# Latent attention: the place of the maxima, the turn, the shift row and the gates

## The chip, the cores and the metric

The kernel runs on one core of one Trainium2 chip. The metric is the device time of one execution in microseconds (us); the reference points are three timed runs and one profiled execution of the kernel before. The engines are TensorE (PE in the profile, its weight loads PEld), VectorE (DVE), ScalarE (ACT), GpSimd (POOL) and SyncE (SP, which here issues DMAs).

## The reference, cut to what matters

A backbone of two layers over 1024 latent and 256 context tokens, model width 1024, float32. Layer 0 is a windowed attention, layer 1 a latent attention with 16 heads. The change touches only layer 1's attention and what follows it:

```python
def attend(qn, qr, kn, kr, v):
    s = (einsum("bqhd,bkhd->bhqk", qn, kn)      # 64 columns of a head
         + einsum("bqhd,bkd->bhqk", qr, kr)) * scale   # 32 rotated columns, keys shared by the heads
    p = softmax(s, axis=-1)
    return einsum("bhqk,bkhd->bqhd", p, v)
...
ox = attend(...)                    # 1024 queries against 1280 keys (context and latent)
yx = (ox * silu(gx)) @ w_out        # the gate, then the projection
x = x + gate_x * yx                 # and a last RMSNorm
```

## The kernel before, in words

Layer 1's attention is cut into 16 units. Unit `i` has one pair of heads (`i // 2`) and one half of the queries (512, `i % 2`). A unit goes over the 1280 keys in ten chunks of 128 (`NT = 10`). Inside a block called `in_order` each engine gets its instructions in the order in which the program issues them; nothing is reordered, so the place of a line in the unit loop is its place in the engine's queue.

For a chunk `c`, `score(c)` (line 1343) makes ten products into two PSUM banks, one for each head: five terms (high and low parts of the keys against the queries, the rotated part, and a last term that also adds the negated maximum of each query through extra rows of `q`). ScalarE takes the exponential of both banks at once (1347) and GpSimd adds it into a running sum `acc` (1351, 1353). The banks are 3 and 4 for even chunks, 5 and 6 for odd ones. `PV` (1360) multiplies five chunks at a time by the values, in two column halves of 64, into bank 7.

The maxima must be known before a unit's first exponential. So unit `nu`, the next one, has its maxima made during unit `u`, from rough scores of the high parts: `nu.top(PIECES[c])` (1305), four products of 512 keys (or eight of 256) into two of the banks 0 to 2, which go round (`topb`), and two reduces on VectorE (1311, 1313). After the last chunk and the last `PV`, `nu.turn` reduces the partial maxima (1316) and transposes them to a row on TensorE (1318), and `nu.shift` spreads that row into `q`: one head on VectorE (1323), the other in four pieces on ScalarE (1330). The turn's bank is 5 (`psd`) if a projection follows, else one of `topb`.

Finishing the unit before (`pu`) lies inside unit `u`: at chunk 5 `fin2` sums `acc` over its partitions on TensorE (1371) and copies it (1373); `fin3(0)` and, after the turn, `fin3(1)` take the reciprocal (1377) and multiply the output by it (1378), each for 256 queries; `fin4` multiplies by the gate on VectorE (1382) and stores the result (1384).

Between units TensorE may get a projection that fills the turn: K of the next pair after units 0, 2, ... 12 (`make_K`, lines 126 to 128, cast on ScalarE at 121, subtracted on VectorE at 122), V of the next four heads after units 3, 7 and 11 (`make_V`, copied by ScalarE at 1257). After units 1, 5, 9, 13 and 14 there is none. These projections use the same banks 0 to 2 (`fillb`, set to `topb`'s place). `nnu.prep` (1290 to 1295) loads the queries of the unit after the next; `fin` (1364, 1366) copies bank 7 out and loads the gate. `wo_fill` cuts pieces of the output weight on ScalarE and GpSimd (121, 122), one a unit, two in units 6, 12 and 13. Behind unit 15 come the output tiles (`out_tiles`), whose first needs unit 14's gated output (`fetch_out`, `cut_out`).

The unit loop before:

```python
if c == 0:
    u.score(0, 0, 4)
    u.score(1, 0, 4)
if c > 1:
    u.score(c)
if nu:
    nu.top(PIECES[c])
if c < 2:
    u.score(c, 4, 5)
```

Of the kernel before, what the change touches and what calls it, by code (L numbers as in the profile page):

```python
# [9 lines left out]
F32 = mybir.dt.float32  # L10
# [49 lines left out]
def kernel(ctx: ExitStack, tc: tile.TileContext, t, out, dbg=None):  # L60
    nc = tc.nc
# [57 lines left out]
    def split(hi, lo, src, lo_eng=None):  # L119

        nc.scalar.copy(hi, src)  # L121
        (lo_eng or nc.vector).tensor_sub(lo, src, hi.bitcast(F32))  # L122
# [1153 lines left out]
    class UnitB:  # L1276
# [38 lines left out]
        def turn(self, bank):  # L1315
            nc.vector.reduce_max(shp(self.mx, 2, 64)[:, :, 32:36], self.mxp, AX.X, negate=True)
            self.pm = bank
            nc.tensor.transpose(self.pm[0:100, 0:128], self.mx[:, 0:100], ident)

        def shift(self, engs):  # L1320
            for r, eng in zip((slice(32, 36), slice(96, 100)), engs):
                if eng is nc.vector:
                    eng.tensor_tensor(
                        shp(self.q[r, 3], 4, 128), self.pm[r, 0:128].unsqueeze(1).to_broadcast([4, 4, 128]),
                        ident[r, r].unsqueeze(2).to_broadcast([4, 4, 128]), ALU.mult,
                    )
                else:
                    for b in range(4):
                        o = self.q[r, 3, b * 128 : b * 128 + 128]
                        eng.activation(o, self.pm[r, 0:128], AF.Copy, scale=ident[r, r.start + b : r.start + b + 1])  # L1330

        def score(self, c, i0=0, i1=5):


            q, kt = self.q, self.kt
            cs = slice(c * 128, c * 128 + 128)
            b = 3 + 2 * (c % 2)
            terms = ((kt, 0, 0, 64), (kt, 0, 1, 64), (kt, 1, 0, 64), (KR, 0, 2, 64), (KR, 1, 3, 36))
            for i in range(i0, i1):
                k, s, sq, n = terms[i]  # L1340
                for e in range(2):
                    r = slice(64 * e, 64 * e + n)
                    nc.tensor.matmul(PB[:, b + e, :], k[r, s, cs], q[r, sq], start=i == 0, stop=i == 4)  # L1343
            if i1 < 5:
                return
            E = self.E[c] = shp(Er.next(), 2, 512)
            nc.scalar.activation(E, PB[:, b : b + 2, :], AF.Exp)  # L1347
            acc = shp(self.acc, 2, 512)
            eng = nc.vector if self.i == NU - 1 and c > 4 else nc.gpsimd
            if c == 1:  # L1350
                eng.tensor_add(acc, self.E[0], E)
            elif c:
                eng.tensor_add(acc, acc, E)  # L1353
# [8 lines left out]
        def fin(self):  # L1362
            self.o = otr.next()
            nc.scalar.copy(self.o, PB[:, 7, :])
            self.gt = glr.next()
            load(out=self.gt.bitcast(F32), in_=g1_d[self.pair, :, self.ts])

        def fin2(self):
            acc = shp(self.acc, 2, 512)
            for e, r in enumerate(HALF):  # L1370
                nc.tensor.matmul(psd[r, :], ones, acc[:, e], start=True, stop=True)  # L1371
            self.rec = self.acc[:, 0:512]
            nc.scalar.copy(self.rec, psd)

        def fin3(self, j):
            js = slice(256 * j, 256 * j + 256)
            nc.vector.reciprocal(self.rec[:, js], self.rec[:, js])
            nc.vector.tensor_mul(self.o[:, js], self.o[:, js], self.rec[:, js])

        def fin4(self, c0=0, c1=512):  # L1380
            cs = slice(c0, c1)
            nc.vector.tensor_mul(self.o[:, cs], self.o[:, cs], self.gt[:, cs].bitcast(F32))
            t0 = self.ts.start
            load(out=og_d[self.pair, :, t0 + c0 : t0 + c1], in_=self.o[:, cs])

# [29 lines left out]
        load(out=x, in_=x1_d[256 + ti * 128 : 384 + ti * 128, :])  # L1415
        return o, x

    def cut_out(f, eng=None):
        o, x = f
        og = shp(ogr1.next(), 2, 8, 128)  # L1420
        for h in range(2):
            hs = slice(4 * h, 4 * h + 4)
            split(og[:, 0, hs], og[:, 1, hs], o[:, hs].bitcast(F32), eng)
        return og, x

    def out_tiles(ready, got):
# [66 lines left out]
    for b in range(4):  # L1493
        for i in range(3):
            units[0].top([(b, i)], (PB[:, 2 * i, :], PB[:, 2 * i + 1, :]))
        next(gs[b])
        next(gs[b])
        if b == 3:
            units[0].turn(psd)
            units[0].shift((nc.vector, nc.vector))  # L1500
        next(gs[b])
        if b == 1:
            units[1].prep()
    nc.scalar.activation(const[:, 1:2], const[:, 1:2], AF.Exp)
    wo_fill = wo_pieces()
    for ui, u in enumerate(units):
# [3 lines left out]
        for c in range(NT):  # L1510
            if c == 5:
                if pu:
                    pu.fin2()
                u.PV(0, 5)
                if pu:
                    pu.fin3(0)
                if pu and nu is None:
                    pu.fin4(0, 256)
                    first = fetch_out(0)
                    pu.fin3(1)  # L1520
                    pu.fin4(256, 512)
# [12 lines left out]
            if nu is None and c == 0:  # L1534
                load2(out=gx1, in_=gate_d[1, 0, :].partition_broadcast(128))
                load2(out=fg, in_=t["final_g"].partition_broadcast(128))
        if nnu:
            nnu.prep()
        u.PV(5, NT)
        if nu:  # L1540
            filled = u.half == 0 and u.pair < 7 or ui % 4 == 3
            nu.turn(psd if filled else topb())
            if pu:
                pu.fin3(1)
# [93 lines left out]
```

## Time and profile before

| | |
|---|---|
| median of 3 runs | 1580.59 us (1579.82 to 1583.61) |
| the profiled execution | 1582.15 us |
| its span, first to last instruction | 1580.3 us |
| mean granted TensorE clock | 0.99 |
| busy: PE, DVE, ACT, POOL | 1522.8, 1015.2, 734.9, 775.4 us |
| the units, first score of unit 0 to the first output tile | 1004.05 to 1485.82 us of the span |

A row of the timeline has the start in us from the start of the span, the duration, the engine, the line, the operation, what it writes and reads, the count, and in brackets how long the engine stood before it and what ended that. Rows that follow each other without a gap are merged, so a row of five adds has the time of all five. The chain of work is followed back from the last instruction; its shares say which engine the end waited for. Busy PE is not PE at its peak: where a stretch of the same products takes longer than elsewhere, PE stood, even if the row shows little idle time.

### The profile page before, as it was taken

What the parts mean: (1) busy time and instruction counts of PE and PEld (TensorE: products, weight loads), DVE (VectorE), ACT (ScalarE), POOL (GpSimd) and SP (SyncE); (2) the same over time, 40 slices, a digit from 0 to 9 for tenths busy, and PEclk for the clock granted to TensorE, in tenths of its full rate; (3) what the DMA queues carried; (4) which work ended last, traced back from release to release, by engine and by line L of the source; (5) the groups of instructions that cost most, each with busy time, mean ns of one, the idle gap of its engine ahead of it and who ended that gap; (6) DMA issues with size and microseconds to landing.
All of it is one profiled execution on the core that took longest, in us unless ns stands there. A gap on an engine that the chain in (4) does not pass through costs nothing.

```text
span 1580.3 us, 24759 instructions
## 1 busy us (share of the span) xinstructions
PE 1522.8 (96%) x9026; PEld 1189.2 (75%) x9026; DVE 1015.2 (64%) x1895; ACT 734.9 (47%) x1433; POOL 775.4 (49%) x722
## 2 busy tenths in 40 slices
PE   6899999989999999998999999999999999999998
PEld 2788888778888888886987888766766666766687
DVE  2666868737767887777725202567678678677644
ACT  2512212238877777776523432344445444544422
POOL 2653446315554434444318340477677677688200
PEclk8999999989999999999999999999999999999999
DMA  8535644473333333316304841401122112111442
GB/s 301 175 118 183 196 144 171 144 223 108 114 111 94 97 94 94 94 55 222 92 16 145 308 129 54 117 15 50 44 68 71 44 44 87 44 45 37 140 160 80
DMA packets 123842, 178.91 MB, mean 113 GB/s; under 512 B 11708, under 2 KB 71996, under 8 KB 123720
## 3 DMA queue, kind: packets, MB, share of 16 engines
q1 hardware_dynamic: 116440, 166.40, 33.2%
q10 hardware_dynamic: 7280, 10.92, 2.3%
q8 instruction: 71, 1.16, 0.3%
q14 instruction: 51, 0.42, 0.1%
HBM read 131.13 MB, written 46.15 MB: 112 GB/s over the span
## 4 chain that ended last, share of the span: by engine, by line
PE 83%; DVE 5%; DMA 3%; POOL 3%; issue 3%; ACT 3%; SPq 0%; POOLq 0%; DVEq 0%; ACTq 0%
PE PB L126 14%; PE PB L127 13%; PE PB L128 13%; PE PB L1343 12%; PE PB L1360 9%; PE PB L1305 5%; PE PB L570 5%; PE PB L560 4%; PE PB L533 2%; PE PB L534 2%; PE PB L1371 1%; DMA arena_f<-a_w_in 1%; DMA arena_f<-x 1%; DVE arena_f L344 1%; POOL arena_r L122 1%
## 5 line engine op out<-in xcount | busy, mean ns | idle before, releaser
L126 PE MATMUL PB<-arena_r 128*128 128x512 f32 (+2 forms) x1312 | 475.7, 363 | 3.4 <-ACT arena_r L205 2.1
L127 PE MATMUL PB<-arena_r 128*128 128x512 f32 (+2 forms) x1312 | 469.5, 358 | 3.2 <-POOL arena_r L727 2.3
L128 PE MATMUL PB<-arena_r 128*128 128x512 f32 (+2 forms) x1312 | 469.2, 358 | 0.2 <-DVE arena_r L122 0.2
L1353 POOL TENSOR_TENSOR arena_f<-arena_f 128x1024 f32<-128x1024 f32 x123 | 294.6, 2395 | 18.8 <-ACT arena_f L1347 11.6
L126 PEld LDWEIGHTS PB<-arena_r 128*128 128x128 f32 x1312 | 250.4, 191 | 48.2 <-issue 6.9
L127 PEld LDWEIGHTS PB<-arena_r 128*128 128x128 f32 x1312 | 249.9, 191 | 37.8 <-POOL arena_r L727 2.8
L128 PEld LDWEIGHTS PB<-arena_r 128*128 128x128 f32 x1312 | 249.6, 190 | 35.4 <-DVE arena_r L122 0.4
L1311 DVE TENSOR_REDUCE krF<-PB 128x1 f32<-128x512 f32 (+1 forms) x264 | 167.2, 678 | 112.2 <-PE PB L1305 111.8
L1347 ACT ACTIVATE arena_f<-PB 128x1024 f32<-128x1024 f32 x160 | 164.3, 1027 | 157.2 <-PE PB L1343 154.5
L1343 PE MATMUL PB<-arena_r 64*128 64x512 f32 (+1 forms) x1600 | 220.0, 395 | 1.0 <-ACT arena_f L1347 0.9
L122 POOL TENSOR_TENSOR arena_r<-arena_f,arena_r 128x512 fp32r<-128x512 f32 x96 | 131.5, 1382 | 166.7 <-ACT arena_r L121 152.8
L1343 PEld LDWEIGHTS PB<-arena_r 64*128 64x128 f32 (+1 forms) x1600 | 159.4, 184 | 41.5 <-issue 13.3
L122 DVE TENSOR_TENSOR arena_r<-PB,arena_r 128x512 fp32r<-128x512 f32 (+2 forms) x215 | 140.1, 663 | 76.8 <-ACT arena_r L121 75.1
L540 DVE CUSTOM_DVE_ANT_0 arena_f<-PB,arena_f,small 128x256 f32<-128x256 f32 (+1 forms) x288 | 145.4, 524 | 32.6 <-PE PB L534 25.7
L121 ACT CAST arena_r<-PB 128x512 fp32r<-128x512 f32 (+2 forms) x215 | 120.0, 565 | 55.2 <-PE PB L560 40.9
L1360 PE MATMUL PB<-arena_f 128*64 128x512 f32 x640 | 143.6, 595 | 0.0
L541 ACT ACTIVATE arena_f<-arena_f,small 128x640 f32<-128x640 f32 (+2 forms) x160 | 118.9, 743 | 27.8 <-DVE small L540 26.7
L570 PE MATMUL PB<-arena_r 128*128 128x512 f32 x336 | 121.8, 438 | 4.7 <-ACT arena_f L581 4.1
L344 DVE SCALAR_TENSOR_TENSOR arena_f<-arena_f,small 128x512 f32<-128x512 f32 x98 | 116.2, 1232 | 3.9 <-DMA arena_f<-ada_w 3.5
L1305 PE MATMUL PB<-arena_r 64*128 64x512 f32 (+1 forms) x768 | 112.3, 360 | 6.5 <-DVE krF L1311 5.8
L1360 PEld LDWEIGHTS PB<-arena_f 128*64 128x64 f32 x640 | 44.4, 137 | 84.3 <-issue 82.0
L560 PE MATMUL PB<-ident,arena_f 128*128 128x128 f32 x672 | 105.8, 274 | 0.4 <-ACT arena_f L541 0.3
(165 smaller groups left out, 1892.8 us busy)
## 6 DMA issues: line engine op xcount, KB each, us to landing
arena_r<-q_d SPq DMA_DIRECT2D x148, 128.0 KB, 2.8
arena_f<-ada_w SPq DMA_DIRECT2D x64, 256.0 KB, 3.2
arena_f<-a_w_in SPq DMA_DIRECT2D x40, 256.0 KB, 3.0
arena_f<-ada_w SPq DMA_DIRECT2D x16, 512.0 KB, 7.2
arena_f<-x SPq DMA_DIRECT2D x16, 512.0 KB, 3.7
q_d<-arena_f SPq DMA_DIRECT2D x16, 512.0 KB, 3.2
qn_d<-arena_f SPq DMA_DIRECT2D x16, 512.0 KB, 5.7
arena_r<-qn_d SPq DMA_DIRECT2D x16, 512.0 KB, 5.8
```

The source lines that it names most:

```text
L122: (lo_eng or nc.vector).tensor_sub(lo, src, hi.bitcast(F32))
L126: nc.tensor.matmul(o, ah, bh, start=first, stop=False)
L127: nc.tensor.matmul(o, al, bh, start=False, stop=False)
L128: nc.tensor.matmul(o, ah, bl, start=False, stop=last)
L560: nc.tensor.transpose(pt[:, h, :], self.Ps[h][:, ci * 128 : ci * 128 + 128], ident)
L570: nc.tensor.matmul(self.pv, V[:, self.chunks[ci], self.g, :], PT[:, s], start=ci == 0 and s == 0, stop=ci == self.m - 1 and s == 1,)
L1305: nc.tensor.matmul(bank[:, o : o + n], self.q[r, s, bs], k[r, 0, n0 : n0 + n], start=s == 0, stop=s == 2)
L1311: nc.vector.reduce_max(self.mxp[:, e, b : b + 1, i], bank[:, 0:n], AX.X)
L1343: nc.tensor.matmul(PB[:, b + e, :], k[r, s, cs], q[r, sq], start=i == 0, stop=i == 4)
L1347: nc.scalar.activation(E, PB[:, b : b + 2, :], AF.Exp)
L1353: eng.tensor_add(acc, acc, E)
L1360: nc.tensor.matmul(PB[r, 7, :], Vq[:, c, h, :], E[:, e], start=c == 0, stop=c == NT - 1)
```

## The change

- Maxima and scores. A unit with a successor begins with the first piece of its successor's maxima, then does its first chunk whole. In chunk `c` from 1 on, the piece stands inside the scores: after the first `CUT[c]` of the five terms.
- The turn: two products with 64 columns each against the identity, in the two column halves, instead of one transpose of 100 columns.
- The shift: both heads on VectorE; ScalarE has no part in it.
- `fin3` is split: `inv(j)` is the reciprocal, `fin3(j)` the product. After the turn the order on VectorE is `inv(1)`, both shifts, `fin3(1)`.
- `fin4` becomes `gate`: the product runs on GpSimd, and it is issued at chunk 1 of the unit after the next (`units[ui - 2]`), so the gate buffers are three instead of two. In unit 15 the gates of unit 14 follow at chunk 5 as before; at the end unit 15's are done by halves.
- Unit 15 uses three pairs of banks in turn for its scores, and bank 2 for the sums of unit 14.
- Two last broadcasts (`gx1`, `fg`) are issued by SP instead of ScalarE.

```diff
-    glr = Ring(R, [30, 112], 512)
+    glr = Ring(R, [30, 112, 150], 512)
+    CUT = (0, 1, 1, 2, 2, 3, 3, 4, 4, 5)
...
-            nc.tensor.transpose(self.pm[0:100, 0:128], self.mx[:, 0:100], ident)
+            for r in HALF:
+                nc.tensor.matmul(self.pm[r, 0:128], self.mx[:, r], ident, start=True, stop=True)
...
+        def shift(self):
+            for r in (slice(32, 36), slice(96, 100)):
+                nc.vector.tensor_tensor(
+                    shp(self.q[r, 3], 4, 128), self.pm[r, 0:128].unsqueeze(1).to_broadcast([4, 4, 128]),
+                    ident[r, r].unsqueeze(2).to_broadcast([4, 4, 128]), ALU.mult,
+                )
...
-            b = 3 + 2 * (c % 2)
+            b = (5, 3, 0)[c % 3] if self.i == NU - 1 else 3 + 2 * (c % 2)
...
+        def inv(self, j):
+            js = slice(256 * j, 256 * j + 256)
+            nc.vector.reciprocal(self.rec[:, js], self.rec[:, js])
...
-        def fin4(self, c0=0, c1=512):
+        def gate(self, c0=0, c1=512):
             cs = slice(c0, c1)
-            nc.vector.tensor_mul(self.o[:, cs], self.o[:, cs], self.gt[:, cs].bitcast(F32))
+            nc.gpsimd.tensor_mul(self.o[:, cs], self.o[:, cs], self.gt[:, cs])
...
-                    pu.fin2()
+                    pu.fin2(psd if nu else PB[:, 2, :])
                 u.PV(0, 5)
                 if pu:
+                    pu.inv(0)
                     pu.fin3(0)
...
             if c == 0:
-                u.score(0, 0, 4)
-                u.score(1, 0, 4)
-            if c > 1:
-                u.score(c)
-            if nu:
-                nu.top(PIECES[c])
-            if c < 2:
-                u.score(c, 4, 5)
+                if nu:
+                    nu.top(PIECES[0])
+                u.score(0)
+            else:
+                u.score(c, 0, CUT[c])
+                if nu:
+                    nu.top(PIECES[c])
+                u.score(c, CUT[c], 5)
+            if c == 1 and ui > 1:
+                units[ui - 2].gate()
...
             nu.turn(psd if filled else topb())
             if pu:
+                pu.inv(1)
+            nu.shift()
+            if pu:
                 pu.fin3(1)
-            nu.shift((nc.vector, nc.scalar))
-            if pu:
-                pu.fin4()
...
-    u.fin2()
-    u.fin3(0)
-    u.fin3(1)
-    u.fin4()
+    u.fin2(psd)
+    for j in range(2):
+        u.inv(j)
+        u.fin3(j)
+        u.gate(256 * j, 256 * j + 256)
```

More of the change, by code (lines that the diff above doesn't have):

```diff
@@ L1317, in turn @@
             self.pm = bank
[L1318 to L1330, printed above, removed]
+            for r in HALF:
[6 more added lines that the diff above has]
+                )
         def score(self, c, i0=0, i1=5):
@@ L1343, in score @@
                     nc.tensor.matmul(PB[:, b + e, :], k[r, s, cs], q[r, sq], start=i == 0, stop=i == 4)
-            if i1 < 5:
+            if i0 == i1 or i1 < 5:
                 return
@@ L1416, in fetch_out, with cut_out @@
         return o, x
-    def cut_out(f, eng=None):
+    def cut_out(f):
         o, x = f
@@ L1499 @@
             units[0].turn(psd)
-            units[0].shift((nc.vector, nc.vector))
+            units[0].shift()
         next(gs[b])
@@ L1534 @@
             if nu is None and c == 0:
-                load2(out=gx1, in_=gate_d[1, 0, :].partition_broadcast(128))
-                load2(out=fg, in_=t["final_g"].partition_broadcast(128))
+                load(out=gx1, in_=gate_d[1, 0, :].partition_broadcast(128))
+                load(out=fg, in_=t["final_g"].partition_broadcast(128))
         if nnu:
```

18 lines of the change are left out of this document (9 added, 9 removed).

## The prediction

> **What bounds the kernel now.** I read the page first (shares and chain), then the timeline of the sixteen attention units engine by engine, because the change touches nothing else.
>
> ```profile
> span 1580.3 us, 24759 instructions
> ...
> PE 83%; DVE 5%; DMA 3%; POOL 3%; issue 3%; ACT 3%; SPq 0%; POOLq 0%; DVEq 0%; ACTq 0%
> ```
>
> TensorE (PE) carries the chain. So only time in which PE itself stands can be won, and the question is where in a unit it stands. Unit 6 starts at 1185.17; the rows are start, duration, engine, line:
>
> ```profile
> 1183.97 0.14 PEld L1360 LDWEIGHTS PB<-arena_f 128*64 128x64 f32 x2 [0.29 <-issue]
> 1184.92 0.13 PEld L1318 LDWEIGHTS PB<-ident,krF 128*100 128x100 f32 x1 [0.81 <-issue]
> 1185.17 2.11 PE L1343 MATMUL PB<-arena_r 64*128 64x512 f32 x16
> 1185.28 0.68 DVE L1323 TENSOR_TENSOR arena_r<-PB,ident 4x512 fp32r<-4x512 f32 x1 [0.33 <-PE PB L1318]
> 1186.00 1.75 DVE L1382 TENSOR_TENSOR arena_f<-arena_f,arena_r 128x512 f32<-128x512 f32 x1
> ...
> 1187.79 2.65 DVE L1311 TENSOR_REDUCE krF<-PB 128x1 f32<-128x512 f32 x4
> ...
> 1188.53 0.72 PE L1305 MATMUL PB<-arena_r 64*128 64x512 f32 x3 [0.32 <-DVE krF L1311]
> ...
> 1194.29 1.08 PE L1371 MATMUL PB<-arena_f,small 128*64 128x512 f32 x4
> ...
> 1198.64 0.14 PEld L1360 LDWEIGHTS PB<-arena_f 128*64 128x64 f32 x2 [0.28 <-issue]
> 1199.59 0.99 PEld L1343 LDWEIGHTS PB<-arena_r 64*128 64x128 f32 x10 [0.81 <-issue]
> ...
> 1207.86 4.51 PE L1360 MATMUL PB<-arena_f 128*64 128x512 f32 x20
> ```
>
> Chunks 5 to 9 (70 score and maxima products) run from 1199.59 to 1207.86: 8.27 us, 0.118 each, with no wait. The same 70 products of chunks 0 to 4 run from 1185.17 to 1194.29: 9.12. The difference, 0.85 us, is the standing time of a unit: the second maxima piece finds its bank not yet reduced (1188.53), because both pieces come close together behind the first 16 score products, and the reduce (1187.79) waits for the gate product (1186.00). Unit 0 shows the same without any gate:
>
> ```profile
> 1004.05 2.12 PE L1343 MATMUL PB<-arena_r 64*128 64x512 f32 x16
> ...
> 1013.18 4.51 PE L1360 MATMUL PB<-arena_f 128*64 128x512 f32 x20
> ```
>
> 9.13. Units 1 to 13 stand alike by this reading (unit 6 is their example); unit 14 is worse (below). So 14 x 0.85 + 1.95 = 13.9 us is all that a new order of maxima and scores can win. I now work out what PE waits for in the new order, per kind of unit. S is the unit's first product.
>
> **What blocks VectorE (DVE).** The normalising product (L1378, 256 wide) and the GpSimd (POOL) adds:
>
> ```profile
> 1174.91 12.29 POOL L1353 TENSOR_TENSOR arena_f<-arena_f 128x1024 f32<-128x1024 f32 x5 [0.66 <-ACT arena_f L1347]
> 1190.69 2.41 POOL L1351 TENSOR_TENSOR arena_f<-arena_f 128x1024 f32<-128x1024 f32 x1 [3.49 <-ACT arena_f L1347]
> ...
> 1195.51 1.28 POOL L122 TENSOR_TENSOR arena_r<-arena_f,arena_r 128x512 fp32r<-128x512 f32 x1
> ```
> ```profile
> 1183.79 1.17 DVE L1378 TENSOR_TENSOR arena_f<-arena_f 128x256 f32<-128x256 f32 x1
> ...
> 1446.31 0.42 DVE L1378 TENSOR_TENSOR arena_f<-arena_f 128x256 f32<-128x256 f32 x1
> ```
>
> With POOL idle it takes 0.42; beside adds it ends 0.2 behind the end of the add that runs. The five adds end at 1174.91 + 12.29 = 1187.20, each 2.46 long, so one ends at 1184.74 and the product at 1184.96. The gate of 1186.00 likewise ends at 1187.75. The single-source and PSUM-fed operations (reciprocal, reduce, shift) show no such stretch. This decides most of what follows: after the change DVE does shift, shift (2 x 0.70), then this product, then the reduce of the first piece.
>
> **POOL's load.** Each unit gains a gate there, behind its first add. Nearest row: 1.28 for a two-source 512-wide operation (1.24 pitch); ends 1.2 (half an add) and 2.4 (a whole one); I take 1.24, same shape. In a unit begun after a K projection, POOL's first add starts 5.5 behind S (1190.69), and the first of the last five waits 0.66 for an exponential (1174.91, unit 5). The gate eats that 0.66, so adds end 1.24 - 0.66 = 0.58 later against PE (a shorter PE wait moves both ends alike).
>
> **Units 2, 6, 10 (nothing between the turn and the unit).** Old adds end at S + 2.03 (1187.20 - 1185.17), now S + 2.6; in unit 2 still 2.03, since unit 1 has no gate. The product is posted at about S + 1.5, behind the add end at S + 0.15, so it ends at S + 2.8. The reduce of the first piece's first half (0.66) ends at S + 3.5, and the second piece's second product, 18th in the new order (S + 2.0 unhindered), stands 1.6. In unit 2: 1.05. Against 0.85: +0.75, +0.75, +0.2 = +1.7. The query loads are hidden here: the maxima now need at S what they needed at S + 1.9.
>
> ```profile
> 1179.65 0.53 SPq L1290 DMA_DIRECT2D arena_r<-qn_d  x1
> ```
> ```profile
> arena_r<-qn_d SPq DMA_DIRECT2D x16, 512.0 KB, 5.8
> ```
>
> Issued 5.52 before S and landing in 5.8, they hold the first piece for 0.3 (four small loads follow; up to 1.2). That ends before the DVE wait does, so it costs nothing unless DVE comes free.
>
> **Units 1, 3, 5, 9, 11 (after a K projection), and 7, 13.**
>
> ```profile
> 1078.62 12.30 POOL L1353 TENSOR_TENSOR arena_f<-arena_f 128x1024 f32<-128x1024 f32 x5 [0.66 <-ACT arena_f L1347]
> ```
> ```profile
> 1092.35 2.11 PE L1343 MATMUL PB<-arena_r 64*128 64x512 f32 x16
> ```
> ```profile
> 1210.79 4.92 POOL L1353 TENSOR_TENSOR arena_f<-arena_f 128x1024 f32<-128x1024 f32 x2
> ```
> ```profile
> 1214.99 0.39 PE L128 MATMUL PB<-arena_r 128*128 128x512 f32 x1
> ...
> 1215.35 1.35 ACT L121 CAST arena_r<-PB 128x512 fp32r<-128x512 f32 x3
> ...
> 1216.02 2.11 PE L1343 MATMUL PB<-arena_r 64*128 64x512 f32 x16
> 1216.29 1.62 DVE L122 TENSOR_TENSOR arena_r<-PB,arena_r 128x512 fp32r<-128x512 f32 x3
> ```
>
> The first piece now follows the projection at once and takes the banks of K blocks 0 and 1, which must first be cast (ACT) and subtracted (DVE). 16 score products used to hide that. Block 1 ends at S - 0.64 (1215.38), its cast (1.35 for 512 + 512 + 256 columns: 0.55) at about S, its subtraction (0.63 of the 1.62) at S + 0.7. Adds end at 1090.92 = S - 1.43, now S - 0.85, so the product ends at S - 0.65 and block 0's subtraction by S. PE stands about 0.65 instead of 0.85; -0.2 x 5 = -1.0. In units 7 and 13, whose predecessors have a second weight piece, adds end at S - 0.31 (1215.71), now S + 0.25. The product is posted at S - 2.0, and the add before ends at S - 2.2. Caught, the unit stands 0.65; missed, the product ends at S + 0.45, two subtractions follow, and it stands 1.65. The two times lie 0.2 apart, less than I can place them: I take the middle, 1.15: +0.3 x 2 = +0.6.
>
> **Units 4, 8, 12 (after a V projection).**
>
> ```profile
> 1250.57 2.11 PE L1343 MATMUL PB<-arena_r 64*128 64x512 f32 x16
> ```
> ```profile
> 1250.68 0.59 ACT L1257 COPY arena_f<-PB 128x512 f32<-128x512 f32 x1 [0.85 <-PE PB L128]
> ```
>
> The piece takes the bank of the last block, copied out at 1251.27 = S + 0.7: 0.65 of standing, -0.2 x 3 = -0.6. **Unit 0** has neither projection nor product ahead: 0, so -0.85.
>
> **Unit 14.**
>
> ```profile
> 1432.51 2.11 PE L1343 MATMUL PB<-arena_r 64*128 64x512 f32 x16
> ...
> 1442.72 1.08 PE L1371 MATMUL PB<-arena_f,small 128*64 128x512 f32 x4
> ```
> ```profile
> 1430.75 4.89 POOL L1353 TENSOR_TENSOR arena_f<-arena_f 128x1024 f32<-128x1024 f32 x2
> ```
>
> 10.21, so 1.95 of standing. Adds end at S + 0.7 and S + 3.13, now S + 1.3 and S + 3.7; the product is posted at S + 1.5. Missed: 2.75. Caught: 0.3. Middle 1.5: -0.4.
>
> **Unit 15** has no maxima.
>
> ```profile
> 1460.98 2.73 PE L1343 MATMUL PB<-arena_r 64*128 64x512 f32 x20
> ...
> 1468.63 1.08 PE L1371 MATMUL PB<-arena_f,small 128*64 128x512 f32 x4
> ```
> ```profile
> 1473.23 2.49 DVE L1382 TENSOR_TENSOR arena_f<-arena_f,arena_r 128x256 f32<-128x256 f32 x1
> ...
> 1483.42 1.14 ACT L121 CAST arena_r<-arena_r 128x512 fp32r<-128x512 f32 x2 [1.71 <-DMA arena_r<-og_d]
> ...
> 1485.82 0.50 PE L126 MATMUL PB<-arena_r 128*128 128x512 f32 x1
> ```
>
> 7.65 against 50 x 0.118 = 5.9; the third bank pair and ACT without its shift leave a wait of 0.5 for the shift: -1.2 on PE. But the first output tile needs unit 14's gate, stored and fetched, 7.7 from gate end (1475.72) to cast (1483.42). On POOL that gate ends behind the fourth add and unit 13's gate, at about S + 15.7 instead of S + 14.7; its tile can start at S + 24.1 instead of 24.84. So about -0.5, bounds -1.2 and +1.
>
> **The turn.** From the last weight load of the values' products to the score it takes 1.20 (1183.97 to 1185.17) with the transpose and 0.95 without (1198.64 to 1199.59): the transpose costs 0.25. Two pairs of 128 columns at a quarter of a 512-column pair (0.43) are 0.22: equal, 0. Ahead of a projection the transpose loaded together with it, so there I add 0.1 x 10 = +1.0; bounds -0.15 and +0.2 for each of 15. A rule of the Trainium skill speaks for a gain instead: TensorEngine Tiling (Array Packing), Key Properties, says that a change of tiling mode drains the engine, and the new turn keeps the 64-column mode of the products ahead of it. By it a drain (8.27 less 70 x 0.115, about 0.16, as an estimate) would go per unit and the sum would be 2.4 lower; the row of 0.25 for transpose and switch together leaves no room for that.
>
> ACT's four shift pieces and the rest of ACT's work are hidden by PE before and after: 0. SP's store of the gate now waits for POOL until about S + 9, but the loads queued behind it serve later units: 0. The two last broadcasts move to SP's queue: 0.
>
> **Sum:** +1.7 - 1.0 + 0.6 - 0.6 - 0.85 - 0.4 - 0.5 + 1.0 = -0.05: nothing. The profiled execution took 1582.15 (span 1580.3 and 1.85 around), 0.1% over the median of 1580.59. On the median: 1580.5. A measurement tells about 0.3%, 4.7 us, from no change.
>
> **Rivals.**
>
> *DVE comes free.* If the product after the shifts is not held by POOL, units 2, 6, 10 and 14 stand for at most 0.3: -0.55 x 3 - 1.65 = -3.3 instead of +1.3, and 7 and 13 cost -0.2 each instead of +0.3: 1580.5 - 4.6 - 1.0 = 1574.9; with the turn's lower bound 1572. For: the 0.42 row. Against: every product beside adds ends with one. The Trainium skill, SBUF — State Buffer, section SBUF: two separate sides, says the same: whichever of GpSimd and a two-input VectorE operation starts first holds the shared ports for its whole instruction. 0.28.
>
> *The first piece waits behind a projection (slower).* If POOL ends 1.1 later than I place it (a gate of 2.3 instead of 1.24), product and two subtractions end at S + 1.7 in units 3, 5, 9 and 11 (unit 1 has no product ahead): four more units at 1.65 instead of 0.65, +4.0. Units 6 and 10 stand 1.1 longer, +2.2; units 7, 13 and 14 then catch the earlier add, -1.2. Together +5.0: 1585.5, with 2 more from the turn 1587.5. Each 0.1 us of POOL costs 0.4 in the four and 0.2 in the two, so it decides from about 1 us on. For: nothing covers the four units, and a gate as long as a whole add is within the bounds above. Against: the 1.28 row. 0.16.
>
> No change has 0.56. The range runs from 1572 to 1587.5: the rivals' ends, which the unknown turn (-2.3 to +3) and the caught or missed adds (-2.2 to +2.2) fill.
>
> **What would show it.** Right: the first half of units 2, 6, 10 longer than 9.12, with a wait of the second piece on the reduce, and the reduce directly behind a long product; after a K projection a wait of the first piece on L122 of DVE; unit 0 at 8.3; the five adds of a unit ending 0.6 later against the next start. Wrong: first halves of 8.3 throughout, or a turn whose gap departs from 1.20 by more than 0.15.

## Result and profile after

The changed kernel takes 1586.8 us (median of 7 runs, 1584.17 to 1588.26) against 1580.59 for the kernel before (7 runs, 1579.75 to 1583.61): ratio 1.0034, 95% interval 1.0022 to 1.0046. It is 5 to 6 us slower, and the interval lies clear of 1. No change was forecast (1580.5); the result lies near the upper end of the range. The profiled execution took 1586.8 us (kernel before: 1582.15).

The page of the changed kernel, its span and its chain of waits, to be laid beside the 1580.3 us and the PE share of 83% of before:

```profile
span 1585.0 us, 24820 instructions
...
PE 79%; DVE 6%; DMA 4%; POOL 4%; issue 3%; ACT 3%; SPq 0%; POOLq 0%; ACTq 0%; DVEq 0%
```

The span is 4.7 longer and TensorE's share of the chain is smaller: TensorE waits more, for VectorE, GpSimd and DMA, a point each. Where it does is read from the timeline, unit by unit. Lines of the changed kernel: turn 1320, shift 1324, pieces 1306, their reduces 1312 and 1314, scores 1340, gate 1382, normalising product 1378. In a TensorE row the bracket is a wait that is over when the row starts. Unit 2, which begins right behind its turn (S = 1060.63):

```profile
1053.30 9.75 POOL L1350 TENSOR_TENSOR arena_f<-arena_f 128x1024 f32<-128x1024 f32 x4
...
1060.63 0.72 PE L1306 MATMUL PB<-arena_r 64*128 64x512 f32 x4
1060.75 1.41 DVE L1324 TENSOR_TENSOR arena_r<-PB,ident 4x512 fp32r<-4x512 f32 x2 [1.52 <-PE PB L1320]
...
1062.19 1.14 DVE L1378 TENSOR_TENSOR arena_f<-arena_f 128x256 f32<-128x256 f32 x1
...
1063.36 2.57 DVE L1312 TENSOR_REDUCE krF<-PB 128x1 f32<-128x512 f32 x4
1064.11 0.73 PE L1306 MATMUL PB<-arena_r 64*128 64x512 f32 x3 [1.13 <-DVE krF L1312]
```

The first piece is done at 1061.35, but its reduce starts at 1063.36: both shifts and the product stand ahead of it, and the product, posted while the last of four adds runs (to 1063.05), ends 0.28 behind that add. The second piece stands 1.13. Units 7 (after a K projection, L122 its subtraction) and 14:

```profile
1212.83 4.85 POOL L1350 TENSOR_TENSOR arena_f<-arena_f 128x1024 f32<-128x1024 f32 x2
...
1215.63 2.33 DVE L1378 TENSOR_TENSOR arena_f<-arena_f 128x256 f32<-128x256 f32 x1
...
1217.99 1.62 DVE L122 TENSOR_TENSOR arena_r<-PB,arena_r 128x512 fp32r<-128x512 f32 x3
1218.74 1.32 PE L1306 MATMUL PB<-arena_r 64*128 64x512 f32 x4 [0.98 <-DVE arena_r L122]
```
```profile
1436.42 4.82 POOL L1350 TENSOR_TENSOR arena_f<-arena_f 128x1024 f32<-128x1024 f32 x2
...
1439.19 2.33 DVE L1378 TENSOR_TENSOR arena_f<-arena_f 128x256 f32<-128x256 f32 x1
...
1441.55 2.57 DVE L1312 TENSOR_REDUCE krF<-PB 128x1 f32<-128x512 f32 x4
1442.30 0.72 PE L1306 MATMUL PB<-arena_r 64*128 64x512 f32 x3 [1.62 <-DVE krF L1312]
```

In both the product is posted about 0.37 after the first of two adds has ended (1212.83 + 2.43 = 1215.26; 1436.42 + 2.41 = 1438.83, taking half of each row) and then waits for the whole second one: 2.33. In unit 13 it comes 0.6 late and takes 2.11. Unit 6 waits for something else, the query load for the next unit's maxima, issued at 1180.03 and landed 6.6 later, when the turn was long over:

```profile
1180.03 0.53 SPq L1291 DMA_DIRECT2D arena_r<-qn_d  x1
...
1186.67 1.53 PE L1306 MATMUL PB<-arena_r 64*128 64x512 f32 x4 [1.07 <-DMA arena_r<-qn_d]
```

Unit 3, after a K projection, waits for the casts and subtractions of the bank that its first piece takes:

```profile
1092.51 0.49 PE L1306 MATMUL PB<-arena_r 64*128 64x512 f32 x1
1092.52 1.02 DVE L122 TENSOR_TENSOR arena_r<-PB,arena_r 128x512 fp32r<-128x512 f32 x2 [0.17 <-ACT arena_r L121]
...
1093.27 0.73 PE L1306 MATMUL PB<-arena_r 64*128 64x512 f32 x3 [0.27 <-DVE arena_r L122]
```

From turn to turn, and in unit 15 from the turn to the first output tile, each unit against the kernel before (us, worked out from the starts in the two timelines; the forecast has its 0.1 for the turn in it):

| units | forecast | measured |
|---|---|---|
| 2, 6, 10 | +1.7 | +0.83 +1.11 +0.69 = +2.6 |
| 1, 3, 5, 9, 11 | -0.5 | +0.9 |
| 7, 13 | +0.8 | +1.29 +0.81 = +2.1 |
| 4, 8, 12 | -0.3 | +0.5 |
| 0 | -0.85 | -0.5 |
| 14 | -0.4 | +0.9 |
| 15 | -0.5 | -0.8 |
| sum | -0.05 | +5.7 |

Unit 0's turn came 0.5 earlier in this execution, which leaves +5.1 at the first output tile (1490.94 against 1485.82).

### The profile page after: what moved, and what is told of

Same layout as the page of the kernel before. It is cut to its first block, busy times and chain, and to the rows that moved or that the text cites. A ratio compares the mean times of both kernels' runs of the same rounds, so it can differ in the third digit from the quotient of the medians.

```text
span 1585.0 us, 24820 instructions
## 1 busy us (share of the span) xinstructions
PE 1524.0 (96%) x9074; PEld 1198.0 (76%) x9074; DVE 1011.3 (64%) x1893; ACT 717.1 (45%) x1373; POOL 795.1 (50%) x740
## 4 chain that ended last, share of the span: by engine, by line
PE 79%; DVE 6%; DMA 4%; POOL 4%; issue 3%; ACT 3%; SPq 0%; POOLq 0%; ACTq 0%; DVEq 0%
PE PB L126 13%; PE PB L127 13%; PE PB L128 13%; PE PB L1340 11%; PE PB L1357 8%; PE PB L570 5%; PE PB L1306 5%; PE PB L560 4%; PE PB L533 2%; PE PB L534 2%; DMA arena_f<-a_w_in 1%; PE PB L1368 1%; DVE arena_f L344 1%; DVE arena_r L122 1%; POOL arena_r L122 1%
## 5 line engine op out<-in xcount | busy, mean ns | idle before, releaser
L1340 PE MATMUL PB<-arena_r 64*128 64x512 f32 (+1 forms) x1600 | 225.3, 394 | 0.2 <-DVE arena_r L1324 0.2
L122 POOL TENSOR_TENSOR arena_r<-arena_f,arena_r 128x512 fp32r<-128x512 f32 x96 | 131.9, 1385 | 168.3 <-ACT arena_r L121 160.3
L1340 PEld LDWEIGHTS PB<-arena_r 64*128 64x128 f32 (+1 forms) x1600 | 172.0, 185 | 30.1 <-issue 13.2
L122 DVE TENSOR_TENSOR arena_r<-PB,arena_r 128x512 fp32r<-128x512 f32 (+2 forms) x215 | 140.0, 662 | 75.2 <-ACT arena_r L121 74.1
L1306 PE MATMUL PB<-arena_r 64*128 64x512 f32 (+1 forms) x768 | 119.0, 359 | 9.6 <-DVE arena_r L122 3.8
```

The source lines that it names most:

```text
L1306: nc.tensor.matmul(bank[:, o : o + n], self.q[r, s, bs], k[r, 0, n0 : n0 + n], start=s == 0, stop=s == 2)
```

## Experiments

Theory A: TensorE stands at the pieces, because what they need (casts, query load, the reduce of the piece before) comes late, above all when the normalising product on VectorE is held by a GpSimd add. Theory B: TensorE's own work grew, by the turn and by switching between pieces and scores. Every ratio is to the kernel before on the same chip, that of the experiments from five rounds; a "first half" is the stretch from S to the sums at chunk 5.

| run | ratio | 95% interval |
|---|---|---|
| the change | 1.0034 | 1.0022 to 1.0046 |
| with the single transpose | 1.0018 | 1.0009 to 1.0026 |
| with the late product | 1.0003 | 0.9994 to 1.0012 |
| with the gate before the first add | 1.0025 | 1.0015 to 1.0035 |
| first piece behind 8 products | 1.0023 | 1.0014 to 1.0031 |
| all pieces 10 products apart | 0.9969 | 0.9958 to 0.9981 |
| the same, late product, transpose | 0.9923 | 0.9910 to 0.9937 |
| the change with the old order | 1.0028 | 1.0017 to 1.0040 |
| the kernel before, pieces spaced | 0.9981 | 0.9972 to 0.9991 |
| 0.9923 kernel, with the turn of the change | 0.9933 | 0.9920 to 0.9946 |
| 0.9923 kernel, with the gate on VectorE | 0.9969 | 0.9958 to 0.9980 |
| 0.9923 kernel, with half the shift on ScalarE | 0.9935 | 0.9922 to 0.9949 |

**The single transpose.**

```diff
-            for r in HALF:
-                nc.tensor.matmul(self.pm[r, 0:128], self.mx[:, r], ident, start=True, stop=True)
+            nc.tensor.transpose(self.pm[0:100, 0:128], self.mx[:, 0:100], ident)
```

> The changed kernel with the one transpose of 100 columns back in place of the two 64-column products; nothing else. Theory A (VectorE comes late to the first piece): the turn is worth at most 0.2 us in each of the ten units before a projection, so 0 to -2 us against the changed kernel (1586.8), and the waits of the first and second piece stay (0.75 us after a projection, 1 to 2 us in units 2, 6, 7, 10, 13, 14). Theory B (TensorE's own work grew: turn and switches between kinds of products): the 0.28 us that the turn's start gained in units after a projection goes in all 15 units: -3 to -4 us.

Measured 1584.89, inside theory A's 0 to -2. Between turns the 15 units take 1.65 less than with the products (+4.83 instead of +6.48): the turn is a part of the loss, not most of it.

**The late product.** The second half of the normalising product moves behind the second piece's reduces of the next unit.

```diff
                     nu.top(PIECES[c])
+                if c == 1 and ui > 1:
+                    units[ui - 2].fin3(1)
                 u.score(c, CUT[c], 5)
...
             nu.shift()
-            if pu:
-                pu.fin3(1)
```

> The changed kernel, but the second half of the normalising product (fin3(1)) stands behind the reduces of the second piece of the unit after, instead of behind the shifts. Theory A: the waits that a product held by GpSimd's adds makes go: in units 2, 7, 13 and 14 0.7 to 1.9 us each, in 10 some 0.5; units after a projection keep the 0.75 us that cast and subtraction cost, and unit 6 its wait for the query load. Together -4 to -6 us: 1581 to 1583. Theory B: within 1 us of 1586.8. If the product is then itself held and the second piece's bank waits behind it, nothing is gained either; its rows would show it.

Measured 1583.59, 4.9 less by the ratios, where 4 to 6 less was expected. The timeline of unit 2 in this run (S = 1062.05):

```profile
1062.17 1.41 DVE L1324 TENSOR_TENSOR arena_r<-PB,ident 4x512 fp32r<-4x512 f32 x2 [1.51 <-PE PB L1320]
...
1063.61 2.57 DVE L1312 TENSOR_REDUCE krF<-PB 128x1 f32<-128x512 f32 x4
...
1066.22 0.42 DVE L1378 TENSOR_TENSOR arena_f<-arena_f 128x256 f32<-128x256 f32 x1
...
1067.21 2.40 POOL L1348 TENSOR_TENSOR arena_f<-arena_f 128x1024 f32<-128x1024 f32 x1 [2.85 <-ACT arena_f L1344]
```

The reduce follows the shifts at once, and the product, now in GpSimd's pause, takes 0.42 instead of 1.14. Unit 2 goes from +0.83 to -0.33, unit 14 from +0.89 to -0.75, unit 7 from +1.29 to +0.17, unit 13 from +0.81 to +0.19. Unit 6 still waits 0.72 for its query load (+0.80). The filled units (those behind a projection) 3, 4, 5, 8, 9, 11 and 12 don't move by more than 0.05, unit 1 loses 0.3 more, for a reason that the rows don't show. Theory A holds for the product, and this part of the loss is 4.9 us between the turns.

**The gate before the first add.**

```diff
-            if c == 1 and ui > 1:
+            if c == 0 and ui > 1:
                 units[ui - 2].gate()
```

> The changed kernel with the gate on GpSimd ahead of the unit's first add (issued at chunk 0) instead of behind it, where GpSimd stands 3 to 7 us idle. Theory A: the last five adds of a unit end 0.6 us earlier against TensorE, so the held product ends earlier: unit 10 -0.5, units 7 and 13 -0.3 to -0.6, unit 14 either -2 or 0: -1 to -3.5 us. Theory B: 0.

Measured 1586.66, as theory B had it. From turn to turn units 0 to 14 sum to +6.37 (+6.48). Unit 7 still stands 0.86, unit 13 0.73, unit 14 1.33: the product misses its add either way, and it takes 2.1 to 2.2 in these three. Unit 15 gains 0.7, unit 7 0.4, and unit 5 loses 0.25; in the time this can't be told.

**The first piece behind eight products.**

```diff
             if c == 0:
+                u.score(0, 0, 4)
                 if nu:
                     nu.top(PIECES[0])
-                u.score(0)
+                u.score(0, 4, 5)
```

> The changed kernel, but a unit begins with four of the five terms of its first chunk (8 products, 0.9 us), then the first piece, then the last term; the other pieces stay inside the scores. Theory A: the 8 products cover cast, subtraction and query load: the first half of units after a projection falls from 9.05 to 8.4 us, units 6 and 10 lose their wait for the load, units 2, 7, 13 and 14 lose 0.9 of what the held product costs: -9 to -12 us, 1575 to 1578, clearly below the kernel before. Theory B: first halves stay at 9.0 and the time within 2 us of 1586.8.

Measured 1586.0, far from that. The timeline of unit 3 in this run:

```profile
1093.79 0.62 PE L1306 MATMUL PB<-arena_r 64*128 64x512 f32 x4
1094.25 0.63 PE L1340 MATMUL PB<-arena_r 36*128 36x512 f32 x4
1094.45 2.57 DVE L1312 TENSOR_REDUCE krF<-PB 128x1 f32<-128x512 f32 x4 [0.65 <-PE PB L1306]
...
1095.19 0.29 PEld L1306 LDWEIGHTS PB<-arena_r 64*128 64x128 f32 x3 [0.52 <-DVE krF L1312]
```

The wait for the casts is gone, but with `CUT[1] = 1` only four score products are left between the first and the second piece (1093.79 and 1094.72), and now the second waits for the first one's reduce. The first half is 8.89 instead of 9.07. That is the kernel before's own trouble: two pieces close together. Where the product was held it got worse: in unit 14 the second piece now stands 2.21 instead of 1.62, and the unit is 2.47 longer than in the kernel before (0.89 in the change). Theory A was right about the wait and wrong in what would be late next; the distance between pieces has to be mended too.

**All pieces ten products apart.** Every piece, the first included, stands behind the fourth term of its chunk.

```diff
-    CUT = (0, 1, 1, 2, 2, 3, 3, 4, 4, 5)
+    CUT = (4, 4, 4, 4, 4, 4, 4, 4, 4, 5)
...
-            if c == 0:
-                if nu:
-                    nu.top(PIECES[0])
-                u.score(0)
-            else:
-                u.score(c, 0, CUT[c])
-                if nu:
-                    nu.top(PIECES[c])
-                u.score(c, CUT[c], 5)
+            u.score(c, 0, CUT[c])
+            if nu:
+                nu.top(PIECES[c])
+            u.score(c, CUT[c], 5)
```

> The changed kernel with every piece of the maxima, the first included, behind the fourth term of its chunk's scores, so that 10 score products lie between any two pieces (the change has the first at the start of the unit, then 12, 10, 12, 10 and so on; the run with only the first piece moved behind 8 products left 4 to the second, and the second then stood 0.52). Theory A (a piece stands when the work on VectorE and ScalarE ahead of it, or the reduce of the piece before it, ends late): the casts, the subtraction and the query load are covered by 8 products, and each reduce by 10. The first halves of units 1, 3, 4, 5, 8, 9, 11 and 12 fall from 9.05 to about 8.4 (-5.2 together), the stands of 0.98 and 0.73 ahead of units 7 and 13 and those of 1.07 and 0.40 for the query load ahead of units 6 and 10 go (-3.2), and units 2, 6, 10 and 14, whose normalising product still stands ahead of the first reduce, keep a stand of 0.5 to 1.5 at the second piece. Together about -9 against the changed kernel: some 1576 to 1578. Theory B (TensorE's own work grew, by the turn and by switching between the pieces and the scores): nothing is won, some 1585 to 1587.

Measured 1576.16, at theory A's figure and against theory B. First halves are 8.31 to 8.42 in the eight filled units, and the query load's waits shrink to 0.19. Units 2, 6 and 10 stay at 9.1 to 9.3, as expected, and unit 14 at 10.43, 2 us above the filled units, where at most 1.5 was expected. In units 7 and 13 the stand ahead of the unit goes, but their first halves are still 9.0 to 9.1: the product takes 2.3 in both, so the subtractions of the first piece's banks come late even behind 8 products. That had not been expected.

**Spaced, with the late product and the single transpose.** The edits of three runs above together.

> The kernel with every piece behind the fourth term of its chunk, and besides the second half of the normalising product issued behind the second piece's reduces, and the single transpose of the kernel before for the turn. Theory A: no piece stands any more, first halves of 8.3 to 8.4 in all of units 0 to 14 against 9.12 before (10.21 in unit 14): about -0.75 x 14 - 1.8 = -12 against the kernel before, some 1570, which would be faster than both kernels. Theory B: the first half of a unit is bound by TensorE's own work, and it stays near the kernel before, 1579 to 1582.

Measured 1568.47, 0.9923: faster than both kernels. The timeline of units 5 and 6 in this run:

```profile
1183.47 0.42 DVE L1377 TENSOR_TENSOR arena_f<-arena_f 128x256 f32<-128x256 f32 x1
1183.82 1.28 DVE L1312 TENSOR_REDUCE krF<-PB 128x1 f32<-128x512 f32 x2
1184.04 2.41 POOL L1347 TENSOR_TENSOR arena_f<-arena_f 128x1024 f32<-128x1024 f32 x1 [2.25 <-DVE arena_f L1377]
...
1193.67 0.62 PE L1306 MATMUL PB<-arena_r 64*128 64x512 f32 x4
1194.13 1.32 PE L1339 MATMUL PB<-arena_r 36*128 36x512 f32 x10
1195.29 0.63 PE L1306 MATMUL PB<-arena_r 64*128 64x512 f32 x4
```

The first half is 8.29 to 8.48 in every unit from 0 to 14, with no wait. A piece and ten score products take 1195.29 - 1193.67 = 1.62, 0.116 each; in the kernel before, where the pieces stand between whole chunks, the same fourteen take 1.61 (1190.47 to 1192.08 in unit 6). Pieces inside the scores cost nothing by themselves, which disposes of theory B's switching.

**The change with the old order.** Only the order of pieces and scores goes back.

```diff
             if c == 0:
-                if nu:
-                    nu.top(PIECES[0])
-                u.score(0)
-            else:
-                u.score(c, 0, CUT[c])
-                if nu:
-                    nu.top(PIECES[c])
-                u.score(c, CUT[c], 5)
+                u.score(0, 0, 4)
+                u.score(1, 0, 4)
+            if c > 1:
+                u.score(c)
+            if nu:
+                nu.top(PIECES[c])
+            if c < 2:
+                u.score(c, 4, 5)
```

> The changed kernel with the order of pieces and scores of the kernel before (16 score products, two pieces, then a chunk and a piece by turns); the turn as two products, the shift on VectorE and the gate on GpSimd stay as changed. Theory A: the pieces stand as in the kernel before (0.85 a unit, unit 14 about 2), because the product and the gate on VectorE there ended at about the same time as the product alone does here; what is left of the change is the turn, about 0.1 to 0.15 in each of ten filled units. About +1 to +2 against the kernel before: 1582 to 1584. Theory B: the turn, the shift and the gate make the loss, and the order none: 1585 to 1587.

Measured 1585.67, not 1582 to 1584 but in theory B's span. Between turns the units sum to +3.93: the turn, with the stretch just ahead of it, +2.0, the first half of unit 14 +1.8. Unit 15 gives 0.76 back; unit 0's turn came 0.94 later than in the kernel before's execution. So the trace gives this kernel +3.2 and the change +5.7, while the times of the two can't be told apart. What was missed is unit 14 (S = 1435.69):

```profile
1436.93 2.38 POOL L1350 TENSOR_TENSOR arena_f<-arena_f 128x1024 f32<-128x1024 f32 x1
1437.25 2.34 DVE L1378 TENSOR_TENSOR arena_f<-arena_f 128x256 f32<-128x256 f32 x1
...
1440.37 0.73 PE L1306 MATMUL PB<-arena_r 64*128 64x512 f32 x3 [1.63 <-DVE krF L1312]
```

The product behind both shifts is posted after an add has begun, and its 2.34 hold the pieces with the old order too.

**The kernel before, with its pieces spaced.** Turn, shift, product and gate as before; the pieces stand behind terms 8, 13, 17, 22, 27, 31, 36, 41, 45 and 50 of the unit's scores.

```diff
+    AT = (8, 13, 17, 22, 27, 31, 36, 41, 45)
...
-            if c == 0:
-                u.score(0, 0, 4)
-                u.score(1, 0, 4)
-            if c > 1:
-                u.score(c)
-            if nu:
-                nu.top(PIECES[c])
-            if c < 2:
-                u.score(c, 4, 5)
+            for i in range(5):
+                if nu and 5 * c + i in AT:
+                    nu.top(PIECES[AT.index(5 * c + i)])
+                u.score(c, i, i + 1)
+            if nu and c == 9:
+                nu.top(PIECES[9])
```

> The kernel before with only the places of the pieces changed: the first behind 16 score products as it was, the other nine spread evenly over the rest of the unit (8 to 10 products apart) and the last at its end; turn, shift, product and gate as before, all on VectorE but half of the shift. Theory A: the second piece's second product then comes at about S + 3.5, when the reduce that now holds it has ended in all units but 14 (about 0.5 left): first halves of 8.3 to 8.4, about -0.75 x 14 - 1.4 = -12, some 1570; the turn, the shift and the gate of the change would then not be needed for a gain at all. Theory B: a first half of 9.1 is TensorE's own work, or VectorE's product and gate hold the pieces wherever they are: -3 at most.

Measured 1577.09 instead of 1570; the size, 3.0 by the ratio, is that of theory B, but the rows are those of theory A and a new wait. In the filled units it does what was expected, if less of it: -0.35 to -0.58 a unit between turns (their first half, 7.9 to 8.1, has one piece fewer in it, so the whole unit is compared). Units 2, 6 and 10 lose 0.44. Unit 6 of this run (S = 1181.90):

```profile
1182.73 1.12 ACT L1331 ACTIVATE arena_r<-PB,ident 4x128 fp32r<-4x128 f32 x4 [4.80 <-DVE arena_r L1324]
...
1183.90 0.97 PE L1344 MATMUL PB<-arena_r 36*128 36x512 f32 x6 [0.57 <-ACT arena_r L1331]
```

The first chunk's last term comes at S + 1.43 and waits for ScalarE's half of the shift until S + 2.0. The kernel before begins with eight products of chunk 0 and eight of chunk 1 and keeps the last terms back; those 16 products hid the shift, which the expectation had not seen.

The last three runs price the change's other parts where no piece stands any more.

**The 0.9923 kernel with the turn as two products.**

```diff
-            nc.tensor.transpose(self.pm[0:100, 0:128], self.mx[:, 0:100], ident)
+            for r in HALF:
+                nc.tensor.matmul(self.pm[r, 0:128], self.mx[:, r], ident, start=True, stop=True)
```

> The kernel with evenly spaced pieces and the late product (1568.5 with the single transpose), with the turn as two 64-column products again, as in the change. Where no piece stands any more, this prices the new turn alone. Theory A (the products cost net 0.13 to 0.2 in each of the ten filled units, 0.3 in unit 0, about nothing in the others): +1.5 to +2.5, some 1570 to 1571. Theory B (the turn's cost was an artefact of the standing pieces behind it, and it is free once they are covered): 1568.5.

Measured 1570.93: +0.0010 in the ratio, 1.6 us, inside theory A's span, but the two intervals overlap. The profiles give the turn the same: +3.4 between turn and S less 1.8 in the stretches ahead of the turn, +1.6. They also differ by 1.1 in the first halves, half of it in unit 6, where the first piece waits twice (0.26 and 0.30) for small loads of the next unit's queries, and that is not the turn's.

**The 0.9923 kernel with the gate on VectorE.**

```diff
-            nc.gpsimd.tensor_mul(self.o[:, cs], self.o[:, cs], self.gt[:, cs])
+            nc.vector.tensor_mul(self.o[:, cs], self.o[:, cs], self.gt[:, cs])
```

> The kernel with evenly spaced pieces, late product and single transpose, with the gate product on VectorE again at the same place (between the reduces of the second and the third piece, where GpSimd's first add becomes ready). This prices the gate on GpSimd. Theory A (of two such operations the one that starts first holds the other): the gate follows the normalising product at once and starts 0.1 to 0.2 ahead of the add, takes about 0.75, and the third piece's reduce has some 0.6 in hand: 0 to +0.2 a unit, 1568 to 1571. Theory B (a product on VectorE beside GpSimd's adds always waits for an add): held 1.5 to 2.4, the fourth piece stands 1 to 1.8 in each of 13 units: 1582 to 1592.

Measured 1576.91: +0.0046, 7.3 us, between the theories. Unit 6 of this run, around the gate (L1381):

```profile
1187.53 0.69 DVE L1381 TENSOR_TENSOR arena_f<-arena_f,arena_r 128x512 f32<-128x512 f32 x1
1187.63 2.83 POOL L1347 TENSOR_TENSOR arena_f<-arena_f 128x1024 f32<-128x1024 f32 x1 [2.81 <-DVE arena_f L1377]
...
1188.13 2.57 DVE L1312 TENSOR_REDUCE krF<-PB 128x1 f32<-128x512 f32 x4
...
1188.87 0.72 PE L1306 MATMUL PB<-arena_r 64*128 64x512 f32 x3 [0.17 <-DVE krF L1312]
```

The mechanism is theory A's: the gate starts 0.1 ahead of the add and takes the 0.69 that it takes alone, and this time the add is the longer one, 2.83 instead of 2.41. The Trainium skill, SBUF — State Buffer, section SBUF: two separate sides, says that of the two the one that starts first has the shared ports for its whole instruction; these rows show it from the other side, though the add loses 0.42 of the 0.59 in which both run, not all of it. The price was wrong: the reduces of the third piece were taken to have 0.6 in hand and have less; the fourth piece waits, and the first halves of units 2 to 14 are 0.41 to 0.65 longer.

**The 0.9923 kernel with half the shift on ScalarE.** One head's row on VectorE, the other in four parts on ScalarE, as in the kernel before.

> The kernel with evenly spaced pieces, late product and single transpose, with the second half of the shift on ScalarE in four parts again, as in the kernel before. This prices the shift on VectorE. Theory A: in the five units that begin right behind the turn (2, 6, 10, 14, 15) the last term of the first chunk's scores comes at about S + 1.4, and ScalarE's four parts end at S + 2.57 (the kernel before with only the pieces spaced stood 0.57 there, from S + 2.0): about 1.1 each, +5.5, 1574; the filled units are unchanged. Theory B: ScalarE's parts are hidden as the prediction had them: 1568.5.

Measured 1571.59: +0.0012, 1.9 us, with overlapping intervals; the rows carry it. Units 2, 6, 10, 14 and 15 lose 0.41 to 0.44 each in their first halves, filled units nothing. Unit 15 (S = 1452.55):

```profile
1454.55 0.74 PE L1344 MATMUL PB<-arena_r 36*128 36x512 f32 x4 [0.57 <-ACT arena_r L1331]
```

The right units and the right wait, but 0.57 long and not 1.1: ScalarE's parts end at S + 2.0. The expectation had read the row of the run before as a wait that begins at S + 2.0; it ends there.

## Why the prediction was wrong

Most of the mechanisms that it named are those that the trace shows; the sum went wrong in four places, all to the same side. The turn's part is contained in the figures of the units, so the four must not be added up.

- **Caught or missed adds (units 7, 13, 14): the step that failed.** The working put the product at S - 2.0 and the add's end at S - 2.2, in unit 14 at S + 1.5 and S + 1.3: missed by its own numbers in all three. It took the middle of both branches because 0.2 was less than it could place. Measured, the product came about 0.37 too late in units 7 and 14 and 0.6 in unit 13, and it missed its add again in these units with the single transpose and with the early gate. The branch "missed" would have given +0.9 (its turn's 0.1 included) for each of units 7 and 13 and +0.8 for unit 14: together +2.6, where the middle gave +0.4. Measured +3.0. So 2.2 of the missing 5.7 lie here, and with them the forecast would have been slower by 2, still within 0.3%. The three were also one question (where do GpSimd's adds lie against the turn?), not three that cancel.
- **Filled units (1, 3, 5, 9, 11 and 4, 8, 12): mis-sized.** Forecast -0.1 each, measured +0.07 to +0.32: together 2.1 more than forecast. The stand behind the projection was right: first halves of 9.05 against 8.42 with the pieces spaced, 0.63 of standing after K where 0.65 was forecast; 9.04 against 8.31, 0.73, after V. Wrong was the floor: it was taken as 8.27, from the second half of a unit, and with the pieces spaced it is 8.3 to 8.5. Why some units have 8.29 and others 8.42 with no wait recorded stays open. The rest is the turn.
- **The turn: forecast +1.0, measured +1.6 to +2.0.** It is 1.65 when it is taken out of the change, 1.6 with the pieces spaced and 2.0 with the old order; in unit 0, where nothing was forecast, it costs 0.3. Where a projection follows, two products take 0.32 from the end of the values' products to the projection, the transpose 0.17. The kernel before, ahead of unit 3's projection:

```profile
1087.68 0.14 PEld L1360 LDWEIGHTS PB<-arena_f 128*64 128x64 f32 x2 [0.28 <-issue]
1088.64 0.13 PEld L1318 LDWEIGHTS PB<-ident,krF 128*100 128x100 f32 x1 [0.81 <-issue]
1088.64 0.32 PE L1318 MATMUL PB<-ident,krF 128*100 128x128 f32 x1
...
1088.71 0.48 PE L126 MATMUL PB<-arena_r 128*128 128x512 f32 x1
```

  The last pair of the values' products ends at 1088.54, two steps of 0.43 behind its weight load at 1087.68, and the projection starts at 1088.71. The changed kernel at the same place:

```profile
1087.66 0.14 PEld L1357 LDWEIGHTS PB<-arena_f 128*64 128x64 f32 x2 [0.29 <-issue]
1088.09 0.14 PEld L1320 LDWEIGHTS PB<-ident,krF 128*64 128x64 f32 x2 [0.29 <-issue]
1088.52 0.39 PE L1320 MATMUL PB<-ident,krF 128*64 128x128 f32 x4
1088.52 0.14 PEld L1320 LDWEIGHTS PB<-ident,krF 128*64 128x64 f32 x2 [0.28 <-issue]
1088.83 0.19 PEld L126 LDWEIGHTS PB<-arena_r 128*128 128x128 f32 x1 [0.17 <-issue]
1088.84 0.49 PE L126 MATMUL PB<-arena_r 128*128 128x512 f32 x1
```

  The products start when the pair before ends (1088.52) and the projection at 1088.84. Without a projection the forecast "equal" held (0.32 against 0.25 and about 0.1 ahead of the transpose). The rule on draining in the Trainium skill (TensorEngine Tiling (Array Packing), Key Properties) would have made the turn a gain: of 2.4 as the working has it, of 3.3 by its own figures, for 8.27 less 70 x 0.115 is 0.22 and not 0.16. The runs show no gain, as the row of 0.25 had suggested.
- **The query load: costed at nothing, with the condition that VectorE is later anyway.** In unit 6 it landed 6.6 after its issue, not 5.8, and stood TensorE for 1.07 at the turn; in units 10 and 14 about 0.4. The wait differs from run to run (in unit 6 it is 0.72 with the late product, none with the single transpose). Unit 2, with no such wait, lost 0.83 instead of 0.2: the adds ended at S + 2.4 instead of the S + 2.03 that the working took over from unit 6 of the kernel before. No gate runs ahead of it, and with the old order and all other edits they end at S + 1.96: it is the new order that moves these adds, and the working had charged the gate alone with that. Units 2, 6, 10 together: 0.9 more than forecast.

Units 0 and 15 had the right sign (-0.5 for -0.85, -0.8 for -0.5). Of the signs of being right, unit 0 at 8.36, the wait on L122 after a K projection and the longer first halves of units 2 and 10 (9.93 and 9.81) came; unit 6 has 9.09, as most of its wait lies ahead of its S. One row was misread without harm: the product at 1446.31 does not have GpSimd idle beside it, for two adds run from 1444.06 to 1448.97 and the first ends at about 1446.4; that it takes 0.42 with GpSimd idle is shown by the run with the late product.

Of the rivals, "DVE comes free" (1574.9) was built by the late product: the product took its 0.42, and units 2, 7, 13 and 14 won 0.6 to 1.65 each against the change, but the load, the turn and the filled units kept it at 1583.6. "The first piece waits behind a projection" gave the right time (1585.5 to 1587.5) by the wrong mechanism: units 3, 5, 9 and 11 did not wait for a later add, and moving the gate on GpSimd changed nothing that the time can tell. That the time came out where this rival had it is luck.

What stays open: the trace gives the old order with the other edits 2.5 less than the change, the times 1 us with overlapping intervals. That the new order by itself made the loss is therefore not shown; that the product, the distance of the pieces and the turn each cost time in the change is, by taking each away. The three pairs of banks in unit 15 and the two moved broadcasts were not tried alone.

## What to carry to other kernels

Put the users of a ring of buffers (here PSUM banks that go round) at even distances: here ten products between two pieces cover a reduce of 1.3 us, four don't, and moving the first piece alone only moves the wait to the second. Place a two-input VectorE operation where GpSimd pauses for a reason of its own (here, the first add waits for exponentials): it then takes 0.42 instead of up to 2.3, and nothing queued behind it is late. When a forecast rests on several near misses with one cause, give them one sign, the one that the central numbers have, and leave the other to the range.

## What the runs showed beyond that

The same parts can lose or win by the order they stand in. Beside evenly spaced pieces and a late product, the gate on GpSimd is worth 7 us, the shift on VectorE 2, and the two-product turn costs 1.6 (the last two rest on the rows, as the intervals of the times overlap); in the change itself these parts came with a loss of 5 to 6. And the exclusion between VectorE and GpSimd works in both directions: an add that starts 0.1 behind a two-input product takes 0.42 longer (2.83 against 2.41).
